# Storing finished tiles from the rows they are added to, and moving a weight tile by 448 bytes, in a four-mixer hybrid layer

## Chip, cores and metric

The kernel runs on one core of one Trainium2 chip. The metric is the device time of one execution in microseconds (us). Three executions of the kernel before took 1055.12 to 1059.49 us, with a median of 1059.02.

## What is computed

One layer over 2,048 tokens of width 1,024, in float32. After an RMS norm a projection gives 13 slices of 256 columns, which four mixers use: dilated attention (A), a gated MLP over chunks (B), pooling (C) and retention (D). Each mixer's output is gated, the four are joined, projected back, normed and added to the input rows:

```python
h = _rms_norm(x, pre_g)
proj = jnp.einsum('bsd,de->bse', h, w_in)
aq, ak, av, ag, bu, bv, bg, cx, cg, dq, dk, dv, dg = jnp.split(proj, N_IN_SLICES, axis=-1)
...
y = jnp.concatenate([ya * jax.nn.silu(ag), yb * jax.nn.silu(bg),
                     yc * jax.nn.silu(cg), yd * jax.nn.silu(dg)], axis=-1)
y = jnp.einsum('bse,ed->bsd', y, w_out)
return x + _rms_norm(y, post_g).astype(x.dtype)
```

## The kernel before

Each float32 product is made of three TensorE matmuls: both operands are split into a high and a low part, and high·high, high·low and low·high are summed in the same accumulator.

**Projections and mixers (0 to 682 us).** The normed rows are transposed into `hh` (high) and `hl` (low), for groups of 512 tokens. `weights()` loads a slice of `w_in` and splits it. Two forms use it. `proj_t` (matmuls into `ps_t`) holds 128 columns of weights in the array and streams 512 tokens of `hh` or `hl`. `proj_m` (into `ps_m`) holds 128 tokens of `hh` or `hl` and streams 256 columns of the weight tile `w256`, in 32 calls of 48 matmuls. `w256` is the first tile of its pool `pa` in the stack of the left side of SBUF; its start there is a multiple of 512 bytes, and the tiles of the pools after it lie behind it.

**Attention (682 to 922 us).** Two pairs of heads. Mixers B, C and D are finished by then, and their outputs lie in DRAM (`yb`). For nine of the 16 tiles of 128 tokens, `partial(t)` already projects these three mixers' six blocks: it loads them as `yraw`, `split_y` makes the stationary tiles `yt` from them, 36 matmuls go into `ps_out`, ScalarE copies the result to `z`, and `z` is stored in DRAM as `partd`. The `issue_after` marks at the end of the program spread the nine calls over the second pair of heads. `yt`, `yraw` and `z` of these calls lie in pool `p3` on the right side of SBUF, which is filled from the top down; there `yt` starts 32 bytes past a multiple of 64, and in `p4` on a multiple of 64.

**Tail (922 us to the end).** `combine` finishes the attention's part (`ya`, and its low and high parts `ysa`). Then `final(t)` runs once for each tile. Tiles 0 to 8 load the stored half sum into `z` (pool `p4`, name `z4`, four buffers), project the remaining two blocks with 12 matmuls, and VectorE adds `z` to the accumulator (L868). Tiles 9 to 15 are projected whole, 48 matmuls. The order is three whole ones, then mixed. For every tile the input rows are loaded into `xr` (three buffers), ScalarE squares and sums (L869), a chain of small VectorE operations gives the reciprocal root, VectorE scales the accumulator into `z` (L875), GpSimd adds the input rows (L877; for the last tile VectorE, in halves), and SyncE stores `z` (L878). The matmuls' stationary blocks `yt` of tile 9 lie in `p3`, those of tiles 10 to 15 in `p4`.

SyncE issues every DMA, in program order: a load that must wait for a buffer holds up all that stand behind it on that queue. The order of each engine's instructions comes from a scheduler that works with estimated durations; pools and their buffer counts set which waits it adds. Where a buffer is written again, the writer waits for the last reader, a store among them.

The two pools' names in the text: `pa` on the left in the projections, `p3` on the right from the attention on. `cp` holds constants, `p2` the attention's small tiles. Two tiles named `align0` and `align1` hold no data and only fill space.

Of the kernel before, what the change touches and what calls it, by code (L numbers as in the profile page):

```python
# [9 lines left out]
F32 = mybir.dt.float32  # L10
# [4 lines left out]
ALU = mybir.AluOpType  # L15
# [3 lines left out]
P = 128  # L19
SEQ = 2048  # L20
DM = 1024
# [67 lines left out]
def hymba(ctx: ExitStack, tc: tile.TileContext, x, pre_g, w_in, sgu_g, sgu_w, sgu_b, pool_w,  # L89
          pool_scale, ret_g, w_out, post_g, cmix, catt, out, dbg=None, npart=9, spread=(0.3, 0.95)):  # L90
    nc = tc.nc
    V, A, G, T, D = nc.vector, nc.scalar, nc.gpsimd, nc.tensor, nc.sync
# [10 lines left out]
    cp = ctx.enter_context(tc.tile_pool(name="const", bufs=1))  # L103
# [15 lines left out]
    ya_d = [scratch(f"ya{g}", [P, 2, GRP]) for g in range(NG)]  # L119

    ident = cp.tile([P, P], F32, name="ident")
    cp.tile([P, 96], F32, name="align0")
    for _ in range(2):
        small.tile([P, 8], F32, tag="align1", name="align1")

# [22 lines left out]
    with ExitStack() as c1:  # L148
# [42 lines left out]
        W2 = 6  # L191
        hT = {}
        first = []

        def prologue(gs, step):

# [43 lines left out]
        def weights(col, n, eng=V, scales=(1.0,)):  # L240

            if n == P:
                w = p1.tile([P, 2, KT, n], F32R, tag="w128", bufs=3, name="w128")
            else:
                w = pa.tile([P, 2, KT, n], F32R, tag="w256", bufs=1, name="w256")
            kc = KT * P // n
            for k in range(0, KT, kc):
                raw = p1.tile([P, kc, n], F32, tag="raw", bufs=2, name="raw")
                D.dma_start(raw, w_src[:, k:k + kc, col:col + n])
                for i, sc in enumerate(scales):  # L250
                    cs = slice(i * n // len(scales), (i + 1) * n // len(scales))
                    hi, lo = w[:, 0, k:k + kc, cs], w[:, 1, k:k + kc, cs]
                    A.activation(hi, raw[:, :, cs], AF.Copy, scale=sc)  # L253
                    if sc == 1.0:
                        eng.tensor_tensor(lo, raw[:, :, cs], r32(hi), ALU.subtract)  # L255
                    else:
                        V.scalar_tensor_tensor(lo, raw[:, :, cs], sc, r32(hi), ALU.mult, ALU.subtract)
            return w
# [301 lines left out]
    def attention(p, tab):  # L560
        o01 = (big if p == 0 else po).tile([P, 2, SEQ], F32, tag="big" if p == 0 else "o01", name="att_o01")
        o2 = po.tile([P, SEQ], F32, tag="o2", name="att_o2")
        o = [o01[:, 0], o01[:, 1], o2]
        wt = pc.tile([P, 3, 2, 2, 2, 8], F32, tag="wt", bufs=1, name="wt")
        for s in range(2):
            h = 2 * p + s
            rows = slice(s * HD, (s + 1) * HD)
            other = slice((1 - s) * HD, (2 - s) * HD)
            q2 = pm.tile([P, SEQ], F32R, tag="m8", bufs=7, name="q2")
            k2a = pm.tile([P, SEQ], F32R, tag="m8", bufs=7, name="k2a")  # L570
            k2b = pm.tile([P, SEQ], F32R, tag="m8", bufs=7, name="k2b")
            D.dma_start(r32(q2[rows]), qk_d[0][p][rows, 0])
            D.dma_start(r32(q2[other]), qk_d[0][p][rows, 1])
            for z in (rows, other):
                D.dma_start(r32(k2a[z]), qk_d[1][p][rows, 0])
                D.dma_start(r32(k2b[z]), qk_d[1][p][rows, 1])
            for b, dil in enumerate(DILS):
                vt = pm.tile([P, 16, 2 * HD], F32R, tag="m8", bufs=7, name="att_v")
                dst = r32(vt)
                if dil == 1:  # L580
                    src = v_d[h].rearrange("(n t c) d -> c t n d", c=4, t=32)
                    for c in range(4):
                        D.dma_start(dst[c * 32:(c + 1) * 32], src[c])
                elif dil == 4:
                    D.dma_start(dst.rearrange("q (j c) d -> q j (c d)", j=4),
                                v_d[h].rearrange("(j q c) d -> q j (c d)", j=4, c=4))
                else:
                    D.dma_start(dst.rearrange("q r d -> q (r d)"), v_d[h].rearrange("(q r) d -> q (r d)", r=16))
                qb = q2
                if dil != 1:  # L590
                    qb = pm.tile([P, SEQ], F32R, tag="m8", bufs=7, name="q2b")
                    if dil == 4:
                        src = r32(q2).rearrange("p (j k c i) -> p c j k i", j=4, c=4, i=8)
                        dst = qb.rearrange("p (j c k i) -> p c j k i", j=4, c=4, i=8)
                        for c in range(4):
                            (V if c < 3 else G).tensor_copy(dst[:, c], src[:, c])
                    else:
                        V.tensor_copy(qb.rearrange("p (r w i) -> p r w i", r=16, i=8),
                                      r32(q2).rearrange("p (w r i) -> p r w i", r=16, i=8))
                if dil == 1:  # L600
                    sv = p2.tile([P, 3, 2, 16], F32, tag="sv", bufs=2, name="sv")
                    raw = p2.tile([64, P], F32, tag="sT", bufs=1, name="sraw")
                    D.dma_start(raw, st_d[h].rearrange("b z (n q) -> (b z n) q", q=P))
                    branch(h, dil, qb, k2a, k2b, vt, tab, o[b], sv[:, b])
                    weigh(sv, raw, wt[:, :, :, s])
                    continue
                st = p2.tile([P, 2, 16], F32, tag="stat", bufs=2, name="att_st")
                branch(h, dil, qb, k2a, k2b, vt, tab, o[b], st)
                keep_stats(h, b, dil, st)
        return o01, o2, wt  # L610
# [203 lines left out]
    def load_y(t, pool):  # L814
        raw = pool.tile([P, 6, P], F32, tag="yraw", bufs=2, name="yraw")
        D.dma_start(raw, yb_d[t // 4][:, t % 4])
        return raw

    def split_y(raw, pool, eng):

        ys = []
        for e in range(0, 6, 3):
            yt = pool.tile([P, 3, 2, P], F32R, tag="yt", bufs=2, name="yt")
            src = raw[:, e:e + 3]
            if eng is A:
                A.activation(yt[:, :, 0], src, AF.Copy)
            else:
                eng.tensor_copy(yt[:, :, 0], src)
            G.tensor_tensor(yt[:, :, 1], src, r32(yt[:, :, 0]), ALU.subtract)
            ys += [yt[:, j] for j in range(3)]  # L830
        return ys
# [12 lines left out]
    def partial(t):  # L844
        z = p3.tile([P, DM], F32, tag="z", bufs=2, name="z")
        ys = split_y(load_y(t, p3), p3, G)
        for n in range(2):
            A.activation(z[:, n * GRP:(n + 1) * GRP], out_proj(ys, range(2, 8), n, ps2, "part"), AF.Copy)
        D.dma_start(part_d[t * P:(t + 1) * P], z)

    def final(t, have, yb, py, p4, ps4, tag, post_b, last):
        tt = slice((t % 4) * P, (t % 4 + 1) * P)
        ys, es = [ya[e][t // 4][:, :, tt] for e in range(2)], (0, 1)
        z = p4.tile([P, DM], F32, tag="z4", bufs=4, name="z4")
        if have:
            D.dma_start(z, part_d[t * P:(t + 1) * P])
        else:
            ys, es = split_y(yb or load_y(t, p4), py, A) + ys, (2, 3, 4, 5, 6, 7, 0, 1)
        xr = p4.tile([P, DM], F32, tag="xr", bufs=3, name="xr")
        D.dma_start(xr, x[0, t * P:(t + 1) * P])  # L860
        ss = small.tile([P, 16], F32, tag="ss", name="ss2")[:, :2]
        sq = p4.tile([P, DM], BF16, tag="sq", bufs=2, name="sq")
        halves = [slice(n * GRP, (n + 1) * GRP) for n in range(2)]
        banks = []
        for n, ns in enumerate(halves):
            ps = out_proj(ys, es, n, ps4, tag)
            if have:
                V.tensor_tensor(ps, ps, z[:, ns], ALU.add)  # L868
            A.activation(sq[:, ns], ps, AF.Square, scale=DM ** -0.5, accum_out=ss[:, n:n + 1])  # L869
            banks.append(ps)  # L870
        V.tensor_scalar(ss[:, :1], ss[:, :1], ss[:, 1:], EPS, ALU.add, ALU.add)
        rstd = small.tile([P, 16], F32, tag="rstd", name="rstd2")[:, :1]
        rsqrt(rstd, ss[:, :1], 1)
        for ps, ns in zip(banks, halves):
            V.scalar_tensor_tensor(z[:, ns], ps, rstd, post_b[:, ns], ALU.mult, ALU.mult)  # L875
        for ns in halves if last else [slice(0, DM)]:
            (V if last else G).tensor_tensor(z[:, ns], z[:, ns], xr[:, ns], ALU.add)  # L877
            D.dma_start(out[0, t * P:(t + 1) * P, ns], z[:, ns])  # L878

    po = ctx.enter_context(tc.tile_pool(name="po", bufs=1, side="right", reuse_waits="tile"))  # L880
    pc = ctx.enter_context(tc.tile_pool(name="pc", bufs=1, side="right", reuse_waits="tile"))
# [64 lines left out]
```

## Time and profile before

| what | value |
| --- | --- |
| time, median of three runs | 1059.02 us (1055.12 to 1059.49) |
| time of the profiled execution | 1055.14 us |
| its span | 1053.4 us |
| its granted TensorE clock, mean | 0.981 of full |
| TensorE busy | 1000.1 us (95%), 5,960 matmuls |
| VectorE busy | 519.1 us (49%) |
| ScalarE busy | 376.4 us (36%) |
| GpSimd busy | 228.0 us (22%) |

All views are of one execution; times in them count from the start of its span. A row of a timeline has its start, its length, the engine, the line of the code, the operation, output and input tiles, the shape and the number of instructions that the row joins; in brackets stands how long the engine was idle before it and what ended the idle time. Matmuls overlap, so the pace of a row of n is its length less that of the last, over n − 1, or the distance of two starts. A row of waits has the total, the number and the longest. SPq is SyncE's queue of DMA issues; a DMA's own row in the chain of work runs from its issue to its landing.

### The profile page before, as it was taken

How to read it: one execution, taken by the hardware profiler on the slowest of the kernel's cores; microseconds unless marked ns; L12 is line 12 of the kernel's file. 1: busy time of each engine (PE TensorE's matmuls, PEld its weight loads, DVE VectorE, ACT ScalarE, POOL GpSimd, SP SyncE). 2: the span in 40 equal slices, each digit the busy share in tenths (PEclk: the TensorE clock that was granted, in tenths of full speed). 3: DMA queues.
4: the chain of work that ended last, by engine and by line, in shares of the span. 5: the costliest groups of instructions: out<-in, count | busy, mean ns of one | idle time of the engine just before them, and what ended most of it. 6: DMA issues, size and time to landing. Idle time of an engine off the chain costs nothing.

```text
span 1053.4 us, 15825 instructions
## 1 busy us (share of the span) xinstructions
PE 1000.1 (95%) x5960; PEld 861.6 (82%) x5960; DVE 519.1 (49%) x1584; ACT 376.4 (36%) x871; POOL 228.0 (22%) x217
## 2 busy tenths in 40 slices
PE   5899999999999999999999999988999989899994
PEld 5889898998888998989898888777896979776773
DVE  7621215687323331031666222176876667727776
ACT  6320313132212431031221111297873878612231
POOL 2310002221133000002120124031116411313444
PEclk9999999999999999999999999996999989989998
DMA  7530222332423232040310661187474663445565
GB/s 284 146 100 21 81 80 81 121 107 72 123 68 103 91 95 65 1 140 34 128 61 21 154 179 41 62 219 203 102 212 141 161 202 77 154 142 181 175 250 220
DMA packets 110988, 128.91 MB, mean 122 GB/s; under 512 B 9888, under 2 KB 88992, under 8 KB 108864
## 3 DMA queue, kind: packets, MB, share of 16 engines
q1 hardware_dynamic: 110912, 127.90, 39.7%
q8 instruction: 47, 0.77, 0.3%
q14 instruction: 29, 0.24, 0.1%
HBM read 91.57 MB, written 36.31 MB: 121 GB/s over the span
## 4 chain that ended last, share of the span: by engine, by line
PE 82%; DMA 7%; DVE 6%; ACT 2%; issue 2%; POOL 1%; SPq 1%; DVEq 0%; POOLq 0%; ACTq 0%
PE ps_t L98 38%; PE ps_m L98 16%; PE ps_out L98 10%; PE ps_s L98 4%; PE ps_o L98 4%; PE ps_pt L101 3%; PE ps_of L98 2%; DMA out_dram<-z 2%; DMA k2b<-qk 2%; DMA cm<-in_cmix_dram 1%; PE ps_in L98 1%; POOL z L877 1%; PE ps_mix L98 1%; DMA raw<-in_w_in_dram 1%; PE ps_x L101 1%
## 5 line engine op out<-in xcount | busy, mean ns | idle before, releaser
L98 PE MATMUL ps_t<-hh,w 128*128 128x512 f32 x1152 | 366.9, 395 | 0.0
L98 PEld LDWEIGHTS ps_t<-hh,w 128*128 128x128 f32 x1152 | 215.9, 188 | 47.8 <-issue 3.4
L98 PE MATMUL ps_t<-hl,w 128*128 128x512 f32 x576 | 226.1, 393 | 0.0
L98 PE MATMUL ps_m<-w,hh 128*128 128x256 f32 x1024 | 190.1, 286 | 1.6 <-ACT hh L235 1.6
L98 PEld LDWEIGHTS ps_m<-w,hh 128*128 128x128 f32 x1024 | 161.3, 193 | 3.3 <-ACT hh L235 2.2
L98 PE MATMUL ps_out<-wo,yt 128*128 128x512 f32 x576 | 153.9, 406 | 0.6 <-DVE z L875 0.6
L98 PE MATMUL ps_m<-w,hl 128*128 128x256 f32 x512 | 147.7, 288 | 0.1
L98 PEld LDWEIGHTS ps_t<-hl,w 128*128 128x128 f32 x576 | 108.3, 188 | 23.2 <-issue 1.4
L98 PEld LDWEIGHTS ps_out<-wo,yt 128*128 128x128 f32 x576 | 105.6, 192 | 23.1 <-issue 2.8
L255 DVE TENSOR_TENSOR w<-raw,w 128x1024 fp32r<-128x1024 f32 x42 | 58.5, 1402 | 109.5 <-ACT w L253 109.5
L98 PEld LDWEIGHTS ps_m<-w,hl 128*128 128x128 f32 x512 | 98.8, 193 | 0.8 <-DVE hl L236 0.3
L253 ACT ACTIVATE w<-raw 128x1024 fp32r<-128x1024 f32 (+1 forms) x56 | 55.0, 997 | 67.7 <-PE ps_t L98 37.3
L652 DVE CUSTOM_DVE_ANT_0 att_p<-ps_s,tab 128x128 f32<-128x128 f32 (+1 forms) x192 | 60.6, 360 | 36.3 <-PE ps_s L98 29.6
L662 DVE TENSOR_TENSOR pt_lo<-ps_pt,pt_hi 128x512 fp32r<-128x512 f32 x80 | 51.5, 652 | 18.6 <-ACT pt_hi L661 18.2
L654 ACT ACTIVATE att_p<-att_p,att_st 128x128 f32<-128x128 f32 (+1 forms) x128 | 55.0, 433 | 6.9 <-DVE att_st L652 6.4
L98 PE MATMUL ps_o<-pt_hi,att_v 128*128 128x128 f32 (+1 forms) x204 | 53.9, 284 | 1.7 <-DVE att_o L677 1.7
L98 PE MATMUL ps_o<-pt_lo,att_v 128*128 128x128 f32 (+1 forms) x204 | 52.9, 294 | 0.4 <-DVE pt_lo L662 0.4
L101 PE MATMUL ps_pt<-ident,att_p 128*128 128x128 f32 x300 | 50.6, 285 | 2.7 <-ACT att_p L654 2.5
L449 POOL TENSOR_TENSOR d_g<-d_g,ret_b 128x512 f32<-128x512 f32 x8 | 10.4, 1296 | 184.6 <-ACT d_g L447 184.6
L661 ACT ACTIVATE pt_hi<-ps_pt 128x512 fp32r<-128x512 f32 x80 | 44.1, 565 | 12.0 <-PE ps_pt L101 6.4
L98 PEld LDWEIGHTS ps_o<-pt_hi,att_v 128*128 128x128 f32 x204 | 41.0, 201 | 4.3 <-DVE att_o L677 1.9
L877 POOL TENSOR_TENSOR z<-z,xr 128x1024 f32<-128x1024 f32 x15 | 35.8, 2390 | 32.4 <-DVE z L875 27.7
(174 smaller groups left out, 1409.9 us busy)
## 6 DMA issues: line engine op xcount, KB each, us to landing
raw<-in_w_in_dram SPq DMA_DIRECT2D x52, 512.0 KB
qk<-qk_s SPq DMA_DIRECT2D x16, 512.0 KB
att_v<-vd SPq DMA_DIRECT2D x8, 1024.0 KB
xr<-in_x_dram SPq DMA_DIRECT2D x16, 512.0 KB
out_dram<-z SPq DMA_DIRECT2D x15, 512.0 KB
xt<-in_x_dram SPq DMA_DIRECT2D x7, 1024.0 KB
yraw<-yb SPq DMA_DIRECT2D x16, 384.0 KB
partd<-z SPq DMA_DIRECT2D x9, 512.0 KB
```

What stands on the lines that cost most here:

```text
L98: return T.matmul(o, lhsT, rhs, start=start, stop=stop, skip_group_check=True)
L101: T.transpose(o, i, ident[:n, :n])
L253: A.activation(hi, raw[:, :, cs], AF.Copy, scale=sc)
L255: eng.tensor_tensor(lo, raw[:, :, cs], r32(hi), ALU.subtract)
L449: G.tensor_tensor(o, o, ret_b.unsqueeze(1).broadcast_to([P, 2, 256]), ALU.mult)
L652: V.tensor_tensor_reduce(out=pr[:, u, :w], in0=ps[:, u, :w], in1=bb, scale=-SLOPES[h] * HD ** -0.5, scalar=3e38, op0=ALU.add, op1=ALU.min, ...
L654: A.activation(pr[:, u, :w], pr[:, u, :w], AF.Exp, bias=neg, scale=-1.0, accum_out=st[:, 1, n:n + 1])
L661: A.activation(hi, pt[:, :w], AF.Copy)
L662: V.tensor_tensor(lo, pt[:, :w], r32(hi), ALU.subtract)
L877: (V if last else G).tensor_tensor(z[:, ns], z[:, ns], xr[:, ns], ALU.add)
```

## The change

Five things are edited. In `final`, the last add writes its result over `xr`, and the store reads `xr`; `xr` gets a fourth buffer. So a `z` buffer is free after the add, and an `xr` buffer only after the store. In `weights`, 448 bytes are reserved ahead of `w256` and 64 behind it: `w256` now starts 448 bytes past a multiple of 512, and what follows it moves by a whole 512. In `partial`, 480 bytes are reserved in `p3` in its first call, by which tiles of `p3` and of the pools behind it on the right side move down; `yt` there now starts on a multiple of 512. The attention's `sv` takes the place of the pad `align0`, of the same size, with one buffer instead of two.

```diff
     ident = cp.tile([P, P], F32, name="ident")
-    cp.tile([P, 96], F32, name="align0")
+    svs = cp.tile([P, 3, 2, 16], F32, name="sv")
...
             else:
+                if not align:
+                    align.append(pa.tile([P, 112], F32, name="align2"))
                 w = pa.tile([P, 2, KT, n], F32R, tag="w256", bufs=1, name="w256")
+                if len(align) == 1:
+                    align.append(pa.tile([P, 16], F32, name="align3"))
...
-                    sv = p2.tile([P, 3, 2, 16], F32, tag="sv", bufs=2, name="sv")
+                    sv = svs
...
         ys = split_y(load_y(t, p3), p3, G)
+        if t == 0:
+            p3.tile([P, 120], F32, name="align4")
...
-        xr = p4.tile([P, DM], F32, tag="xr", bufs=3, name="xr")
+        xr = p4.tile([P, DM], F32, tag="xr", bufs=4, name="xr")
...
-            (V if last else G).tensor_tensor(z[:, ns], z[:, ns], xr[:, ns], ALU.add)
-            D.dma_start(out[0, t * P:(t + 1) * P, ns], z[:, ns])
+            (V if last else G).tensor_tensor(xr[:, ns], z[:, ns], xr[:, ns], ALU.add)
+            D.dma_start(out[0, t * P:(t + 1) * P, ns], xr[:, ns])
```

Up to the last microseconds of the attention every engine keeps its order of instructions. From there on, SyncE's queue has another. This is SyncE early in the tail, before; the number in a name tells the tiles of one name apart, in the order in which they are made, `z4` is `z` of `final`, and the tiles stored are those of the first finals:

```order
L878 DMA out_0_dram<-z4_9119 128x1024
L860 DMA xr_9379<-in_x_dram 128x1024
L878 DMA out_0_dram<-z4_9205 128x1024
L860 DMA xr_9426<-in_x_dram 128x1024
L816 DMA yraw_9883<-yb3_76 128x768
L856 DMA z4_9377<-partd_77 128x1024
L856 DMA z4_9424<-partd_77 128x1024
L856 DMA z4_9471<-partd_77 128x1024
```

And the same place now (the `xr` load of the fourth tile, `xr_9378`, stands 9 rows ahead of the first row shown):

```order
L885 DMA out_0_dram<-xr_9125 128x1024
L821 DMA yraw_9882<-yb3_76 128x768
L867 DMA xr_9425<-in_x_dram 128x1024
L885 DMA out_0_dram<-xr_9211 128x1024
L867 DMA xr_9472<-in_x_dram 128x1024
L863 DMA z4_9376<-partd_77 128x1024
L863 DMA z4_9423<-partd_77 128x1024
L863 DMA z4_9470<-partd_77 128x1024
```

Before, the three `z` loads need the stores of `z4_9119`, `z4_9205` and a later one; now they need adds only, but `xr_9425` ahead of them is loaded into the buffer of `xr_9125`, and `xr_9472` into that of `xr_9211`, both of which are stored just before.

This is SyncE's queue shortly before its end, before the change; only the last stores follow:

```order
L860 DMA xr_9891<-in_x_dram 128x1024
L878 DMA out_0_dram<-z4_9788 128x1024
L860 DMA xr_9972<-in_x_dram 128x1024
L856 DMA z4_9970<-partd_77 128x1024
L856 DMA z4_10017<-partd_77 128x1024
L878 DMA out_0_dram<-z4_9835 128x1024
L860 DMA xr_10019<-in_x_dram 128x1024
L878 DMA out_0_dram<-z4_9882 128x1024
L860 DMA xr_10073<-in_x_dram 128x1024
```

And now:

```order
L867 DMA xr_9890<-in_x_dram 128x1024
L867 DMA xr_9971<-in_x_dram 128x1024
L885 DMA out_0_dram<-xr_9789 128x1024
L867 DMA xr_10018<-in_x_dram 128x1024
L863 DMA z4_9969<-partd_77 128x1024
L885 DMA out_0_dram<-xr_9836 128x1024
L863 DMA z4_10016<-partd_77 128x1024
L885 DMA out_0_dram<-xr_9890 128x1024
L867 DMA xr_10072<-in_x_dram 128x1024
```

The names shift by one (`z4_9970` is now `z4_9969`). Before, the two last `z` loads follow one another, behind one `xr` load, and `z4_10017` takes the buffer of `z4_9788`. Now `xr_10018` takes the buffer of `xr_9789`, whose store stands right ahead of it, and a store lies between the two `z` loads.

More of the change, by code (lines that the diff above doesn't have):

```diff
@@ L193, in hymba @@
         first = []
+        align = []
         def prologue(gs, step):
```

## The prediction

> **What bounds the kernel now.** I read the head of the page first, then the chain of work that ended last, then a table of busy time by stage, and only then single waits.
>
> ```profile
> span 1053.4 us, 15825 instructions
> PE 82%; DMA 7%; DVE 6%; ACT 2%; issue 2%; POOL 1%; SPq 1%; DVEq 0%; POOLq 0%; ACTq 0%
> core 0: us, PE busy (x) PEld busy (x) DVE busy (x) ACT busy (x) POOL busy (x), PEclk, DMA share, GB/s
> 265.00:450.00 185.00, 184.82 (x1024) 160.19 (x1025) 49.77 (x68) 44.96 (x65) 23.64 (x31) 1.00 0.26 76
> 724.00:922.00 198.00, 187.66 (x1227) 166.02 (x1226) 146.07 (x498) 144.64 (x434) 57.93 (x65) 0.97 0.53 151
> 955.00:1054.00 99.00, 79.97 (x344) 63.09 (x342) 70.92 (x229) 23.16 (x68) 43.78 (x23) 0.95 0.60 215
> ```
>
> Three stages with three limits. In the projections (265 to 450 as a sample) TensorE is busy 184.82 of 185 us: whatever one matmul gains or loses there is gained or lost by the kernel. In the attention (724 to 922) it is busy 187.66 of 198. In the tail of output projections (955 to 1054) it is busy 80 of 99 and no engine is full, so there the waits decide. The waits of that stretch, and its end:
>
> ```profile
> DVE ps_out L868 <- DMA z<-partd: 15.7, 5, 5.8
> PE ps_out L98 <- DVE z L875: 3.4, 4, 2.0
> 1039.63 0.39 PE L98 MATMUL ps_out<-wo,ysa 128*128 128x512 f32 x1
> 1036.66 1.30 DVE L868 TENSOR_TENSOR ps_out<-ps_out,z 128x512 f32<-128x512 f32 x2 [5.07 <-DMA z<-partd]
> 1038.47 1.30 DVE L868 TENSOR_TENSOR ps_out<-ps_out,z 128x512 f32<-128x512 f32 x2 [0.52 <-DMA z<-partd]
> 1042.16 1.41 DVE L875 SCALAR_TENSOR_TENSOR z<-ps_out,rstd,post_b 128x512 f32<-128x512 f32 x2
> 1047.39 1.41 DVE L875 SCALAR_TENSOR_TENSOR z<-ps_out,rstd,post_b 128x512 f32<-128x512 f32 x2
> 1048.71 1.28 DVE L877 TENSOR_TENSOR z<-z,xr 128x512 f32<-128x512 f32 x2
> ```
>
> The last matmul is done at 1040.0, yet the span ends 13.4 us later. VectorE sat 5.07 us until the stored half sum of a tile (`z<-partd`) was back at 1036.66; from there it works nearly without a gap (adds, reciprocal roots, scalings, last adds) until 1050, and the last store ends the span. So the end hangs on when that load of `z` lands. Why it landed so late stands on the queue:
>
> ```profile
> 1028.87 0.34 SPq L878 DMA_DIRECT2D out_dram<-z  x1
> 1029.25 2.14 SPq L860 DMA_DIRECT2D xr<-in_x_dram  x1
> 1031.48 2.00 SPq L856 DMA_DIRECT2D z<-partd  x2
> 1033.58 0.38 SPq L878 DMA_DIRECT2D out_dram<-z  x1
> 1028.87 4.24 DMA out_dram<-z
> ```
>
> SyncE issues all transfers in program order. The two `z` loads begin at 1031.48, and the second can only follow when the store issued at 1028.87 has landed (28.87 + 4.24 = 1033.11), as its buffer is that store's source. The first took 1036.66 − 1031.48 = 5.2 us to land, the second 1038.47 − 1033.1 = 5.4.
>
> **The change part by part.**
>
> *Stores from `xr`.* Now the add frees `z`, and only the store's landing frees `xr`. The `z` load itself therefore no longer waits for a store, but the `xr` load does, and in the new program each pair of `z` loads is queued behind an `xr` load that needs the latest store landed. At the end the order becomes: store of tile A (the one issued at 1028.87), `xr` load into A's own buffer, first `z` load, store of the next tile, second `z` load. The `xr` load cannot go before 1033.11. Its own issue takes what such a row takes when nothing holds it:
>
> ```profile
> 1034.01 0.42 SPq L860 DMA_DIRECT2D xr<-in_x_dram  x1
> 1043.70 4.83 POOL L877 TENSOR_TENSOR z<-z,xr 128x1024 f32<-128x1024 f32 x2 [9.59 <-DVE z L875]
> 1031.72 2.39 POOL L877 TENSOR_TENSOR z<-z,xr 128x1024 f32<-128x1024 f32 x1 [0.34 <-DVE z L875]
> ```
>
> So the first `z` load goes at 1033.5 instead of 1031.48, and by 5.2 us lands at 1038.7 instead of 1036.66: +2.0. The second stands behind the store of the tile whose add GpSimd ends at 1031.72 + 2.39 = 1034.1, goes at 1034.5 and by 5.4 lands at 1039.9 instead of 1038.47: +1.4. VectorE needs both in turn, hence between +1.4 and +2.0 at the end. Against that, what comes before may be early: the loads of the first four `xr` rows are issued before the tail begins, and the first three `z` loads are then free of stores of their own. Of VectorE's 15.7 us of waiting for `z` some would go, and only as far as TensorE, 80 of 99 us busy, is not at once in the way again. A gain there is bounded by the wait that an early `z` hands on to TensorE, the 3.4 us row, of which I give half to the four loads that are ahead: −1.7. I take **+1.5**, with −1.7 to +3.4 (a second round of +1.4 on top of +2.0) as bounds. Same work, same instruction shapes: the add writes another buffer, at GpSimd's 2.4 us as before.
>
> *Start of the weight tile in `pa`.* `w256` is the moving operand of `ps_m`. Its start goes from a multiple of 512 bytes to 448 past one; the tiles behind it all move by a whole 512. Count and pace:
>
> ```profile
> L98 PE MATMUL ps_m<-w,hh 128*128 128x256 f32 x1024 | 190.1, 286 | 1.6 <-ACT hh L235 1.6
> L98 PE MATMUL ps_m<-w,hl 128*128 128x256 f32 x512 | 147.7, 288 | 0.1
> 383.29 41.73 PE ps_t L98 x184
> 425.02 23.03 PE ps_m L98 x192
> ```
>
> 1,536 such matmuls at 23.03 / 192 = 120 ns each, in a stage that TensorE fills. The neighbour `ps_t`, twice as wide, takes 41.73 / 184 = 226.8. The difference of the two is 106.8 ns for 256 columns; what is left, 13.2 ns, is the same in both, although `ps_t` streams a tile at another place. So the row shows a fixed cost and none of the start: **0**. Bounds: if the new start brought it to half of a `ps_t`, 113.4 ns, −6.6 × 1,536 = −10.1 us; if it cost what a start off the grid costs in the next item, 8 ns, +12.3 us.
>
> A rule that bears on the size of that gain is in the Trainium skill, "TensorE: Matmul & The Clock Gate", section Back-to-back issue gap: columns over 2.4 GHz and about 2.5 ns, so some 109 ns for 256 columns. The 120 ns here do not agree; by the page the gain could be an estimated 11 ns × 1,536 = 17 us, if the start were what keeps `ps_m` from it.
>
> *480 bytes in `p3`.* All tiles of the right side but the first few move down by 480 bytes; `yt`, the stationary operand of the half sums, from 32 past a multiple of 64 to a multiple of 512.
>
> ```profile
> 913.92 4.42 PE L98 MATMUL ps_out<-wo,yt 128*128 128x512 f32 x18
> 957.04 4.28 PE L98 MATMUL ps_out<-wo,yt 128*128 128x512 f32 x18
> 993.43 4.24 PE L98 MATMUL ps_out<-wo,yt 128*128 128x512 f32 x18
> L98 PE MATMUL ps_out<-wo,yt 128*128 128x512 f32 x576 | 153.9, 406 | 0.6 <-DVE z L875 0.6
> ```
>
> Taking 0.39 us for the last of each run, as the row at 1039.63 has it, the first (a half sum, `yt` in `p3`) goes at (4.42 − 0.39) / 17 = 237 ns, the other two (`yt` in `p4`, on the grid already) at 229 and 226.5. The middle one, like the first, starts behind narrow matmuls, so 8 to 10 ns are the start's. Of the 576, six tiles of 36 lie in `p4`; 360 are in `p3`: 360 × 8 = −2.9 us if all of it lies on the path. 198 − 187.66 = 10.3 us of idle in that stage says that not all does. I take **−2.0**, bounds 0 and −3.8.
>
> The same skill, "SBUF — State Buffer", section Who interferes with whom, gives TensorE two independent read ports, one for the moving operand and one for weight loads, and says that it never waits on anyone. By that the place of `yt` would cost nothing and this term would be 0; 237 against 229 ns speaks for the term.
>
> *Small ones, 0.*
>
> ```profile
> 687.19 1.03 POOL L891 CAST sel<-sel_raw 32x1024 fp32r<-32x1024 f32 x1 [27.38 <-ACT att_p L654]
> 692.15 0.95 POOL L828 CAST yt<-yraw 128x384 fp32r<-128x384 f32 x2 [3.93 <-DMA yraw<-yb]
> ```
>
> `sv` in one buffer: a head fills it only when the head before it has long been weighed, on VectorE in order; without that cover it would be one wait per head. GpSimd's copy of `sel` gets two more waits, on transfers; it ends at 688.2 and GpSimd then idles 3.93 us for a load, which hides them. The fourth `xr` buffer adds no instruction.
>
> **The sum.** 1055.14 us, the time of the profiled execution (its span 1053.4 and 1.7 around it), + 1.5 − 2.0 + 0 = 1054.6. That execution was the fast end of the three shown; the median lies 3.9 higher, at 1059.02. The same step from there is **1058.5 us**. About 0.5%, 5.3 us, is what a measurement of this kernel can tell from no change, so this is no change. Adding the bounds without the weight tile's gives −5.5 to +3.4, 1053.5 to 1062.4.
>
> **The rivals.**
>
> *A, the tail gets shorter.* Two rows for its price, a scaling and the last square:
>
> ```profile
> 1044.65 1.40 DVE L875 SCALAR_TENSOR_TENSOR z<-ps_out,rstd,post_b 128x512 f32<-128x512 f32 x2
> 1040.99 0.60 ACT L869 ACTIVATE sq<-ps_out 128x512 bf16<-128x512 f32 x1
> ```
>
> If the freed `z` buffers let the last two loads land before TensorE ends, VectorE's chain starts not at 1036.66 but with the last matmul: from the end of the last tile's matmuls at 1040.0, one square (0.6), the root and the scaling, which from one tile's scaling to the next's are 1047.39 − 1044.65 = 2.74, then scaling, adds and store as now (1053.4 − 1047.39 = 6.0): 1049.3, −4.1, and up to 3.4 more when TensorE's waits go as well: −4 to −7.5, with the `yt` term −6 to −9.5: about 1051. For it: the 15.7 us of waits. Against: the queue is in order, and an `xr` load that needs a store still stands ahead of them. 25%.
>
> *B, the weight tile's old start is what holds `ps_m`.* −10.1, with the other terms −10.6: 1048. For it: the 13 ns that no column explains, and that `yt` shows a start to matter at all. Against: `ps_t` has the same 13 ns. 10%.
>
> *C, the new wait of the `xr` loads decides (slower).* VectorE waits for `z` in five stretches; if in each the `z` loads go 2.0 us later, as worked out for the last, and TensorE's eight accumulators are full by then so that nothing is caught up, that is 5 × 2.0 = +10.0, with the `yt` term +8.0: 1067. It decides from the point at which TensorE's 3.4 us of waits for the scaling grow with every round. For it: the order of the queue. Against: TensorE has 19 us of slack in that stretch. 12%.
>
> *D, the new start of the weight tile costs (slower).* +12.3 − 0.5: 1071. For it: `yt`'s 8 ns. Against: 448 is a multiple of 64, which `yt`'s old place was not. 8%.
>
> **How the numbers follow.** Forecast 45%, A 25%, B 10%, C 12%, D 8%. Faster by over 0.5% is A and B, 35%; within 0.5% the forecast, 45%; slower C and D, 20%. The range leaves out less than two in ten: at 1046 it cuts off the better half of B, 5%; at 1066 D and half of C, 14%. The forecast's own range is 1053.5 to 1062.4.
>
> **What would show it.** `ps_m` in the chain at 23.0 us for 192 (21.8 would be B, 24.6 D). Half sums' runs of 18 at 4.28 instead of 4.42. In the tail, each `z` load's issue right behind an `xr` load that stood until a store landed, VectorE's last wait for `z` ending about 2 us later against the last matmul, and its total near 15.7 us: under 8 would be A, over 22 C. The forecast is wrong if `ps_m`'s pace moves by over 2 ns, or if TensorE's end and the span's end come closer than 9 us.

## The result, and the profile after

The changed kernel takes 1050.76 us, the median of five runs (1048.79 to 1052.46), against 1059.02 for the kernel before; the ratio is 0.9928, with a 95% interval of 0.9905 to 0.9951. So it is faster by 8 us, 0.7%. The forecast was no change, 1058.5 us, in a range of 1046 to 1066. The time lies in that range, but below the 1053.5 to 1062.4 that the forecast's own terms span.

The profiled execution took 1048.79 us, its span 1047.1, 6.3 us shorter than that of before. Where these 6.3 us lie is read from the first and last start of three groups of matmuls. First the kernel before (duration least, median and most in ns, then first and last start in us):

```profile
L98 PE MATMUL ps_t<-hh,w x1152: 386/390/792, 47.2 to 681.4; 128*128 128x512 f32 x192
L98 PE MATMUL ps_o<-pt_lo,att_v x204: 222/280/416, 689.0 to 913.8; 128*128 128x128 f32 x54, 128*128 128x256 f32 x48
```

The same groups of the changed kernel, and its span:

```profile
span 1047.1 us, 15841 instructions
L98 PE MATMUL ps_t<-hh,w x1152: 387/389/791, 46.8 to 675.9; 128*128 128x512 f32 x192
L98 PE MATMUL ps_o<-pt_lo,att_v x204: 220/279/415, 683.5 to 906.7; 128*128 128x128 f32 x54, 128*128 128x256 f32 x48
```

The projections run from 46.8 to 675.9 instead of 47.2 to 681.4: 5.1 us less. The attention takes 906.7 − 683.5 = 223.2 instead of 224.8: 1.6 less. The tail, from there to the end, takes 1047.1 − 906.7 = 140.4 instead of 139.6: 0.8 more. Attention and tail are near the forecast's −2.0 and +1.5, but differences of this size say little: in the kernel with only the weight tile moved (below) the same two stretches take 223.0 and 141.8 us, though nothing in them was edited. The projections were forecast at 0.

What moved in the projections stands in the chain of work. The prediction shows one run of 192 of the kernel before, 23.03 us; the next one there is this:

```profile
471.54 23.23 PE ps_m L98 x192
```

The changed kernel, same places:

```profile
93.64 22.61 PE ps_m L98 x192
139.71 21.97 PE ps_m L98 x192
379.92 41.73 PE ps_t L98 x184
421.65 22.61 PE ps_m L98 x192
467.72 21.97 PE ps_m L98 x192
```

`ps_t` has kept its 226.8 ns. `ps_m` went from 23.03 to 22.61 us in one run of 192, 2.2 ns a matmul, and from 23.23 to 21.97 in the next, 6.6 ns. From start to start, all runs that long have 120.0 ns before; now some have 117.8 and some 113.4. The mean over all `ps_m` matmuls that follow one another falls from 119.8 to 115.8, which is 6 us in 1,536; 5.1 of them show in the stage.

The end of the tail, by queue, VectorE and TensorE, and the wait that the prediction named:

```profile
1019.40 0.34 SPq L885 DMA_DIRECT2D out_dram<-xr  x1
1023.22 0.33 SPq L867 DMA_DIRECT2D xr<-in_x_dram  x1
1023.64 0.38 SPq L863 DMA_DIRECT2D z<-partd  x1
1024.11 0.38 SPq L885 DMA_DIRECT2D out_dram<-xr  x1
1024.55 0.42 SPq L863 DMA_DIRECT2D z<-partd  x1
...
1029.17 1.30 DVE L875 TENSOR_TENSOR ps_out<-ps_out,z 128x512 f32<-128x512 f32 x2 [6.08 <-DMA z<-partd]
1031.27 0.21 DVE L878 TENSOR_SCALAR ss<-ss 128x1 f32<-128x1 f32 x1 [0.80 <-ACT sq L876]
1032.08 1.29 DVE L875 TENSOR_TENSOR ps_out<-ps_out,z 128x512 f32<-128x512 f32 x2
1041.05 1.41 DVE L882 SCALAR_TENSOR_TENSOR z<-ps_out,rstd,post_b 128x512 f32<-128x512 f32 x2
1042.37 1.28 DVE L884 TENSOR_TENSOR xr<-z,xr 128x512 f32<-128x512 f32 x2
...
1031.22 0.84 PE L98 MATMUL ps_out<-wo,ysa 128*128 128x512 f32 x3
...
DVE ps_out L875 <- DMA z<-partd: 15.9, 3, 7.1
```

This is the mechanism of the first term, row by row. A store is issued at 1019.40; SyncE then stands until 1023.22, for the `xr` load behind it wants that store's buffer and waits for its landing; only then do the two `z` loads go, with a store between them. VectorE waits 6.08 us for the first. SyncE's waits for stores from 955 us to the end, first before and then now (total, number, longest), say the same:

```profile
SPq L856 <- DMA out_dram<-z: 5.3, 4, 1.7
SPq L867 <- DMA out_dram<-xr: 32.3, 12, 4.7
```

Before, four loads of `z` waited for stores, 5.3 us in all; now twelve loads of `xr` do, 32.3 us in all.

The last matmul ends at 1032.1 and the span 15.0 us later, where it was 13.4: 1.6 us more. From the second of the two last adds to the end of the span it is 15.0 us in the changed kernel (1032.08 to 1047.1) and 14.9 before (1038.47 to 1053.4). So the 1.6 us are that add: it starts with the end of the last matmul, where it started 1.5 us ahead of it before. Its load is not the whole reason. By the completion marks of the trace, the second `z` load landed at 1031.5, 0.5 us ahead of the last matmul's end, against 1.6 us before (1038.4): 1.1 us of the 1.6. The rest is VectorE's own order, which has changed here too: the first tile's root steps, which waited 0.80 us for ScalarE's square, now stand between the two adds.

### The profile page after: what moved, and what is told of

The parts are those of the page before. It is cut to its first block, busy times and chain, and to the rows that moved or that the text cites. A ratio compares the mean times of both kernels' runs of the same rounds, so it can differ in the third digit from the quotient of the medians.

```text
span 1047.1 us, 15841 instructions
## 1 busy us (share of the span) xinstructions
PE 991.7 (95%) x5960; PEld 855.2 (82%) x5960; DVE 516.9 (49%) x1584; ACT 376.0 (36%) x871; POOL 229.9 (22%) x217
## 4 chain that ended last, share of the span: by engine, by line
PE 81%; DMA 9%; DVE 5%; POOL 2%; issue 1%; ACT 1%; SPq 1%; DVEq 0%; ACTq 0%; POOLq 0%
PE ps_t L98 38%; PE ps_m L98 15%; PE ps_out L98 13%; PE ps_s L98 3%; PE ps_o L98 3%; PE ps_of L98 2%; PE ps_pt L101 2%; DMA k2b<-qk 2%; DMA ret_b<-in_ret_g_dram 1%; PE ps_in L98 1%; DMA ya<-ysa 1%; DMA wo_raw<-in_w_out_dram 1%; DVE z L882 1%; DMA z<-partd 1%; PE ps_mix L98 1%
## 5 line engine op out<-in xcount | busy, mean ns | idle before, releaser
L98 PE MATMUL ps_m<-w,hh 128*128 128x256 f32 x1024 | 184.3, 282 | 1.8 <-ACT hh L236 1.8
L98 PEld LDWEIGHTS ps_m<-w,hh 128*128 128x128 f32 x1024 | 157.5, 189 | 3.6 <-ACT hh L236 2.4
L98 PE MATMUL ps_m<-w,hl 128*128 128x256 f32 x512 | 145.5, 284 | 0.2 <-DVE hl L237 0.2
L884 POOL TENSOR_TENSOR xr<-z,xr 128x1024 f32<-128x1024 f32 x15 | 37.9, 2533 | 34.2 <-DVE z L882 21.6
```

What stands on the lines that cost most here:

```text
L98: return T.matmul(o, lhsT, rhs, start=start, stop=stop, skip_group_check=True)
L884: (V if last else G).tensor_tensor(xr[:, ns], z[:, ns], xr[:, ns], ALU.add)
```

## Experiments

Every ratio is against the kernel before, executed in the same session on the same chip. It is an estimate over all executions, 4 to 12 of each edited kernel and 12 to 23 of the kernel before, and differs a little from the quotient of the two medians.

| run | median us | before | ratio, 95% interval |
| --- | --- | --- | --- |
| weight tile's start alone | 1050.97 | 1057.62 | 0.9941, 0.9918 to 0.9965 |
| right side and sv | 1051.83 | 1057.62 | 0.9955, 0.9935 to 0.9974 |
| stores from xr alone | 1055.00 | 1057.62 | 0.9981, 0.9960 to 1.0002 |
| weight tile and right side, no stores from xr | 1047.34 | 1058.47 | 0.9901, 0.9873 to 0.9929 |
| weight tile by 256 bytes | 1059.67 | 1058.47 | 1.0008, 0.9988 to 1.0028 |
| hh, hl and wo by 64 bytes | 1050.12 | 1058.47 | 0.9926, 0.9902 to 0.9951 |
| the changed kernel again | 1050.71 | 1058.47 | 0.9939, 0.9911 to 0.9967 |
| sv alone | 1053.92 | 1059.42 | 0.9951, 0.9934 to 0.9968 |
| changed, z loads on ScalarE | 1044.18 | 1059.42 | 0.9855, 0.9828 to 0.9881 |
| weight tile by 192 and right side | 1047.17 | 1059.42 | 0.9886, 0.9862 to 0.9911 |
| weight tile and sv | 1049.44 | 1056.13 | 0.9928, 0.9899 to 0.9956 |

Wherever the right side or `hh` and `hl` move, `sv` is in the constants as well. The groups that are compared differ in their granted clock as well. Among the executions of the kernel before, 0.001 more of it goes with about 0.7 us less (0.71 and 0.73 us in the two groups of 23). The nine executions with `sv` alone have a mean of 0.9796 and those of before beside them 0.9769; the four with the `z` loads on ScalarE have 0.9828. Whether the edits raise the clock or the executions had it by chance is not shown. If it was chance, an estimated 2 us of the gain of `sv` and 4 us of that of the `z` loads go with it.

The theory at the start was that the weight tile's new place brought the gain, with the tail as forecast; the rival, that the freed `z` buffers in the tail brought it.

**The weight tile alone.**

```diff
+                if not align:
+                    align.append(pa.tile([P, 112], F32, name="align2"))
                 w = pa.tile([P, 2, KT, n], F32R, tag="w256", bufs=1, name="w256")
+                if len(align) == 1:
+                    align.append(pa.tile([P, 16], F32, name="align3"))
```

> Only the weight tile's start moves, by 448 bytes. Theory (the start sets the pace of the 1,536 ps_m matmuls): the two runs of 192 in the chain at 22.6 and 22.0 us as in the changed kernel instead of 23.0 and 23.2, the attention begins 5.5 us earlier, the time falls by 5 to 6 us (ratio 0.9945). Rival (the stores from xr brought the gain): ps_m at 120 ns, time within 1 us of before.

It has the changed kernel's pace, 22.61 and 21.97 us, and 0.9941, 6.2 us less; the attention begins 4.5 us earlier, where 5.5 was expected. The theory stands: this one edit is most of the gain.

**The right side, with sv.**

```diff
-    cp.tile([P, 96], F32, name="align0")
+    svs = cp.tile([P, 3, 2, 16], F32, name="sv")
...
+        if t == 0:
+            p3.tile([P, 120], F32, name="align4")
```

> Only the 480 bytes on the right side, with sv in the pad's place, without which they do not fit. Theory: nothing moves up to 682 us, half sums' matmuls at 227 to 229 ns instead of 234 to 237, the attention stage 1 to 2 us shorter, the time 1 to 2.5 us less (ratio 0.998 to 0.999). Rival (the place of yt costs nothing): no difference in the attention stage beyond 0.5 us.

0.9955, 4.8 us less, more than either theory had. The half sums became faster, here a run of 18 in the kernel with the right side moved:

```profile
910.19 4.32 PE L98 MATMUL ps_out<-wo,yt 128*128 128x512 f32 x18
```

(4.32 − 0.39) / 17 = 231 ns instead of 237, some 2 us in 360. These quotients hold the longer first step of a run. From start to start, all half-sum matmuls of the stage that follow one another go from 232.8 to 230.0 ns, which is 1.0 us in 360; 227 to 229 was expected. The rest was put down to `sv`, which the prediction had at nothing; see below.

**The stores from xr alone.**

```diff
-        xr = p4.tile([P, DM], F32, tag="xr", bufs=3, name="xr")
+        xr = p4.tile([P, DM], F32, tag="xr", bufs=4, name="xr")
...
-            (V if last else G).tensor_tensor(z[:, ns], z[:, ns], xr[:, ns], ALU.add)
-            D.dma_start(out[0, t * P:(t + 1) * P, ns], z[:, ns])
+            (V if last else G).tensor_tensor(xr[:, ns], z[:, ns], xr[:, ns], ALU.add)
+            D.dma_start(out[0, t * P:(t + 1) * P, ns], xr[:, ns])
```

> Only the stores from xr and its fourth buffer. Theory: nothing changes up to 914 us; in the tail the loads of xr wait for stores instead of the loads of z, and the end comes 0 to 1.5 us later against the last matmul of the attention (ratio 1.000 to 1.0015). Rival (the freed z buffers brought the gain): time 4 to 7 us less (ratio 0.994 to 0.996).

0.9981, with an interval that just holds 1: 2 us less, if anything, so neither the theory's cost nor the rival's gain is shown. The order of SyncE's queue is not that of the changed kernel: the last `z` loads stand ahead of the last `xr` loads here. That the same edit makes another order when `sv` is moved as well is what the later runs turn on.

**Starts alone.** A stream of matmuls in the kernel's pattern, one moving and one stationary start after another.

```python
for t2 in range(2):
    for j in range(2):
        tt = slice((t2 * 2 + j) * P, (t2 * 2 + j + 1) * P)
        o = acc[:, j * 256:(j + 1) * 256]
        for k in range(8):
            mm(o, hv[0][:, k, tt], wv[:, 0, k], k == 0, False)
            mm(o, hv[0][:, k, tt], wv[:, 1, k], False, False)
            mm(o, hv[1][:, k, tt], wv[:, 0, k], False, k == 7)
```

> A stream of matmuls alone: it leaves out the whole layer and stores zeros and one accumulator. Groups of 96 with 256 moving columns and of 72 with 512, in the kernel's pattern of three, at one moving and one stationary start after another, and all once more in reverse order. Theory A (the start of the moving rows alone): 256 columns at 120 ns with starts that are multiples of 512, 113 to 118 ns at 448, whatever the stationary start; theory B (the distance of the two reads): 448 with 448 as slow as 0 with 0, and stationary starts move the pace as moving ones do; theory C (what ran before sets a phase): the two passes over the same start differ as much as the starts do.

The table of busy time for ten stretches of 10 us shows how many matmuls touch each. In order, as moving start and stationary start in bytes: with 256 columns 192 and 0, 256 and 0, 448 and 0, 512 and 0, 0 and 64, 448 and 448; with 512 columns 0 and 0, 448 and 0, 0 and 32, 448 and 448:

```profile
114.55:124.55 10.00, 10.00 (x90) 1.00 0.00 0
125.79:135.79 10.00, 10.00 (x85) 1.00 0.01 2
161.01:171.01 10.00, 10.00 (x86) 1.00 0.00 0
184.35:194.35 10.00, 10.00 (x85) 1.00 0.01 2
219.12:229.12 10.00, 10.00 (x90) 1.00 0.00 0
265.04:275.04 10.00, 10.00 (x85) 1.00 0.00 0
276.88:286.88 10.00, 10.00 (x45) 1.00 0.01 2
395.34:405.34 10.00, 10.00 (x44) 1.00 0.00 0
446.74:456.74 10.00, 10.00 (x44) 1.00 0.01 2
531.60:541.60 10.00, 10.00 (x45) 1.00 0.01 2
```

The starts of single matmuls give the pace more finely (ns from start to start, past the first 24 of a group, the two passes together; the very first group of the run, 143.9 ns, is left out):

| moving, stationary start | 256 columns | 512 columns |
| --- | --- | --- |
| 0, 0 | 120.0 | 226.7 |
| 256, 0 and 0, 256 | 120.0 (first alone) | 226.7 |
| 448, 448 | 120.0 | 226.7 |
| 64, 0 | 117.8 | 228.9 |
| 128, 0 | 120.0, then 118.6 | 232.4 |
| 0, 64 | 113.3 | 233.3 |
| 192, 0 | 113.3 | not run |
| 448, 0 | 117.8 | 233.3 |
| 0, 448 | 113.3 | 229 |
| 0, 32 | 118.4 | 233.3 |

Theory B: the start of neither operand counts by itself, but the distance of the two, modulo 256 bytes. At distance 0, the narrow matmuls have their worst pace and the wide ones their best: 448 with 448 is as 0 with 0. At other distances the stream shows that the distance alone does not settle the narrow pace: 192 with 0 and 960 with 0 gave 113.3 and 448 with 0 gave 117.8, each in both passes, though all three are 192 modulo 256. Most starts gave the same in both passes; 16 with 0 gave 113.3 and 118.7, as theory C would have it. What settles the rest is not shown.

**Two tests of that in the kernel.** The weight tile by 256 bytes, still at distance 0:

```diff
+                    align.append(pa.tile([P, 64], F32, name="align2"))
                 w = pa.tile([P, 2, KT, n], F32R, tag="w256", bufs=1, name="w256")
+                    align.append(pa.tile([P, 64], F32, name="align3"))
```

> Only the weight tile moves, by 256 bytes instead of 448. Theory B (the distance of the moving and the stationary start, counted modulo 256): ps_m stays at 120 ns, 23.0 and 23.2 us for 192, time within 1 us of before (ratio 0.999 to 1.001). Theory A (any start off a multiple of 512 helps): 22.0 to 22.6 us for 192 and 5 us less.

It changed nothing, 1.0008, and the chain has the old pace to the last digit:

```profile
426.21 23.03 PE ps_m L98 x192
472.72 23.23 PE ps_m L98 x192
```

And the weight tile where it was, but `hh` and `hl` by 64 bytes:

```diff
-    cp.tile([P, 96], F32, name="align0")
+    cp.tile([P, 16], F32, name="align5")
+    svs = cp.tile([P, 3, 2, 16], F32, name="sv")
...
+    small.tile([P, 56], F32, tag="align6", name="align6")
```

> The weight tile's start stays where it was, modulo 512; instead hh and hl, and with them the output weights that follow in the same buffers, move by 64 bytes (sv in the constants, to make room). They are the stationary side of ps_m and the moving side of ps_t. Theory B (the distance decides): ps_m at 113 to 118 ns although its moving start is unchanged (21.8 to 22.6 us for 192), and ps_t, whose distance was 0, slower, 228.9 instead of 226.7 (184 in 42.1 us instead of 41.7), so -3.4 to -10.2 on ps_m, +3.9 on ps_t and +0.9 on the output projections: -5 to +1.5 us. Theory A (the moving start alone): ps_m at 120 ns, and ps_t slower all the same: +5 us.

```profile
94.67 21.78 PE ps_m L98 x192
380.82 42.11 PE ps_t L98 x184
422.93 22.61 PE ps_m L98 x192
```

The narrow matmuls became faster though their moving start is the old one, and the wide ones slower, 42.11 / 184 = 228.9 ns, the stream's number. Theory A falls. The time, 0.9926, is 8 us less, beyond the expected −5 to +1.5; this kernel has `sv` in the constants too.

**Adding up, and the tail.** Both moves without the stores from `xr` (the changed kernel with the lines below as they were before), and the changed kernel on the same chip:

```diff
-        xr = p4.tile([P, DM], F32, tag="xr", bufs=4, name="xr")
+        xr = p4.tile([P, DM], F32, tag="xr", bufs=3, name="xr")
...
-            (V if last else G).tensor_tensor(xr[:, ns], z[:, ns], xr[:, ns], ALU.add)
-            D.dma_start(out[0, t * P:(t + 1) * P, ns], xr[:, ns])
+            (V if last else G).tensor_tensor(z[:, ns], z[:, ns], xr[:, ns], ALU.add)
+            D.dma_start(out[0, t * P:(t + 1) * P, ns], z[:, ns])
```

> Both moves, of the weight tile and of the right side, without the stores from xr. Theory (the two starts add up and the stores from xr cost something beside them): ps_m's runs of 192 at 22.6 and 22.0 us, half sums at 227, time 8 to 9 us under before (ratio 0.9915 to 0.9925), 1 to 2 us under the changed kernel in the same call. Rival (the stores from xr bring 1.5 to 2 us here as well): 1.5 to 2 us over the changed kernel.

> The changed kernel once more, on the same chip and in the same rounds as the kernel with both moves but without the stores from xr. Its ratio to before should come out near 0.993 again. If the stores from xr cost time once the rest is faster, this kernel is 1 to 2 us slower than the one without them; if they save time, as their single run hints (ratio 0.9981, 0.9960 to 1.0002), it is 2 us faster.

Without the stores from `xr` the kernel takes 1047.34 us, with them 1050.71: 3.4 us more by the medians. The two intervals overlap, but the ends of the profiled executions do not. This is the span without the stores from `xr`, and its last matmuls:

```profile
span 1044.9 us, 15824 instructions
1033.62 0.84 PE L98 MATMUL ps_out<-wo,ysa 128*128 128x512 f32 x3
```

The end comes 10.5 us after the last matmul, against 15.0 and 15.3 in the two profiled executions of the changed kernel. The next run takes the supposed cause away: the changed kernel with the `z` loads on ScalarE's queue.

```diff
-            D.dma_start(z, part_d[t * P:(t + 1) * P])
+            A.dma_start(z, part_d[t * P:(t + 1) * P])
```

> The changed kernel, with the nine loads of the half sums into z issued by ScalarE instead of SyncE, so that they no longer stand behind the loads of xr that wait for stores; all else on SyncE keeps its order. Theory (the z loads behind the waiting xr loads are what the stores from xr cost): VectorE's wait for z falls from 15.9 us to under 8, the end comes 11 to 13 us after the last matmul instead of 15.4 to 15.7, time 2 to 4 us under the changed kernel (ratio to before 0.990 to 0.992). Rival (the transfers themselves are late, whoever issues them): ratio 0.993 to 0.995 as before, and the wait stays over 12 us.

```profile
1016.36 0.35 ACTq L863 DMA_DIRECT2D z<-partd  x1
1017.84 0.33 ACTq L863 DMA_DIRECT2D z<-partd  x1
1026.59 1.29 DVE L875 TENSOR_TENSOR ps_out<-ps_out,z 128x512 f32<-128x512 f32 x2 [2.17 <-DMA z<-partd]
1038.33 1.28 DVE L884 TENSOR_TENSOR xr<-z,xr 128x512 f32<-128x512 f32 x2
1031.66 0.84 PE L98 MATMUL ps_out<-wo,ysa 128*128 128x512 f32 x3
DVE ps_out L875 <- DMA z<-partd: 7.5, 3, 3.2
```

The last two `z` loads go at 1016.36 and 1017.84 instead of 1023.64 and 1024.55, VectorE's wait for `z` is 7.5 us (15.9 in the one profile of the changed kernel, 9.2 in the other), and the span, 1043.0, ends 10.5 us after the last matmul (1032.5) instead of 15.0. The ratio is 0.9855, against 0.9928 and 0.9939 for the changed kernel, measured apart from it: some 8 us less, more than the 2 to 4 expected, of which the granted clock may hold a part. So it is the place of the `z` loads in the queue that costs the changed kernel its longer end. This version beats the kernel before and the changed one. That the early `z` buffers are worth anything beyond that is not shown: the end, 10.5 us, is that of the kernel without the stores from `xr`, the two intervals overlap, and `z` loads on ScalarE with the old stores were not run.

**sv.** Its edit alone, and beside the weight tile's:

```diff
-    cp.tile([P, 96], F32, name="align0")
+    svs = cp.tile([P, 3, 2, 16], F32, name="sv")
...
-                    sv = p2.tile([P, 3, 2, 16], F32, tag="sv", bufs=2, name="sv")
+                    sv = svs
```

> Only sv in the pad's place with one buffer, which the prediction priced at nothing. No start of a matmul operand moves, but the queue of SyncE in the tail gets another order by it: the last half sum's store and an output weight's load go behind three loads of xr, and ya0 ahead of them. Theory (the order brought what the two moves do not explain): the end comes 11 to 12 us after the last matmul instead of 13.3, time 1.5 to 2.5 us under before (ratio 0.9975 to 0.9985), with the half sums still at 234 to 237 ns. Rival (it is nothing, and the right side's move alone made 4 us): within 0.5 us of before.

> The weight tile's move and sv in the pad's place; the right side stays and the stores stay with z. Between the weight tile's move alone (0.9941 of before) and both moves with sv (0.9901). If sv's order is worth the 3 to 5 us that its own run hints, and the right side 0 to 1 us: ratio 0.990 to 0.991. If sv is worth 1 to 2 us and the right side 2 to 3: 0.992 to 0.993. The half sums at 234 to 237 ns and the end 11 to 12 us after the last matmul in either case.

Alone it gives 0.9951, 5.2 us less, over twice what was expected. Beside the weight tile it gives 0.9928 against 0.9941 without, 1.4 us less; with the clock's share taken off, as above, the two would be an estimated 3.3 and 2.6. From the other side, the right side's move is worth 0.9955 against 0.9951 beside `sv` alone, nothing, and 0.9901 against 0.9928, 2.9 us, where the weight tile has moved as well. The intervals are 0.2 to 0.3% each way: what is shown is that `sv`'s edit is not free of effect, between 1 and 5 us, and that with the right side it brings 4 to 5. What the two share is an order: with `sv` in the constants the last half sum's store and a load of output weights stand behind three `xr` loads in SyncE's queue, and no start of an operand has moved. Before, and with `sv` alone:

```profile
919.00 0.32 SPq L849 DMA_DIRECT2D partd<-z  x1
919.42 0.38 SPq L553 DMA_DIRECT2D wo_raw<-in_w_out_dram  x1
921.19 1.81 SPq L860 DMA_DIRECT2D xr<-in_x_dram  x3
...
917.76 1.58 SPq L860 DMA_DIRECT2D xr<-in_x_dram  x3
920.85 0.33 SPq L849 DMA_DIRECT2D partd<-z  x1
921.53 0.33 SPq L553 DMA_DIRECT2D wo_raw<-in_w_out_dram  x1
```

The profiled execution with `sv` alone shows little of a gain: the end came 12.5 us after the last matmul instead of 13.4, where 11 to 12 was expected, and that execution, at 1056.5 us, was the slowest of its nine. The other profiled executions bear out a shorter end: 10.5 to 11.6 us in the five further kernels with `sv` in the constants and stores from `z`, 12.8 to 13.4 in the three without (the kernel before, the weight tile alone, the weight tile by 256). In the two pairs of kernels that differ by `sv` alone it is 0.9 and 1.3 us; where the rest of what the medians say comes from stays open.

**The weight tile by 192.**

```diff
-                    align.append(pa.tile([P, 112], F32, name="align2"))
+                    align.append(pa.tile([P, 48], F32, name="align2"))
```

> Both moves without the stores from xr, the weight tile 192 bytes past a multiple of 512 instead of 448. The same distance modulo 256, so by theory B the same choice of two paces, 113.3 or 117.8 ns: 21.8 to 22.7 us for 192, time within 2 us of the kernel with 448 (ratio to before 0.988 to 0.992). If 192 is the better start, as the stream alone had it (113.3 against 117.8), 21.8 us in all four runs of 192 and 3 us less.

0.9886, with the same 22.61 and 21.97 us for 192 as at 448. The same distance modulo 256, the same two paces; the stream's 113.3 at 192 is had in some runs of the kernel only, as at 448. What chooses between 113.3 and 117.8 was not found.

## Why the prediction failed where it did

**The whole.** The range held, the reason did not. The forecast was no change, within 0.5%; the time fell by 0.7%, and `ps_m`'s pace moved by 2.2 and 6.6 ns, over the 2 ns at which the prediction called itself wrong. The time came within 1 us of rival A's "about 1051", but not by its mechanism: A's shorter tail did not come, and half of rival B's gain did. That the sum of the other terms came out near is luck in part, as said below.

**The weight tile: 0 forecast, −5.1 measured.** The step that failed is "what is left, 13.2 ns, is the same in both […]. So the row shows a fixed cost and none of the start". That the remainder is the same in both is no finding: the 106.8 ns for 256 columns was itself taken as the difference of the two paces, and so 120.0 − 106.8 and 226.8 − 2 × 106.8 must be equal, whatever the paces are. Nothing in the rows could tell a fixed cost from one of the start. What the runs showed in its place: both forms ran at the pace of distance 0 from their stationary operand, `ps_m` with its worst, 120.0, and `ps_t` with its best, 226.7; at the new start `ps_m` has 113.4 and 117.8. The range's lower bound for it, −10.1, held: that was 113.4 ns throughout, and the kernel has it about half the time. Rival B, with a chance of 10%, was so nearest to the mechanism, at half its size; what holds `ps_m` is the distance from the stationary start, not the weight tile's start alone.

The argument against rival D, that 448 is a multiple of 64 and `yt`'s place was not, was the wrong ground for the right side: a distance of 64 bytes, or of 448, costs the wide matmuls 2.2 to 6.6 ns in the stream.

**The skill's rule.** The Trainium skill, "TensorE: Matmul & The Clock Gate", section Back-to-back issue gap, gives some 109 ns for 256 columns, by a formula that it calls that of an isolated matmul; of a stream of weight loads and matmuls, which `ps_m` is, it says that both set the spacing, and so the estimate of 17 us took the formula further than the Trainium skill does. The best that any start gave here was 113.3 ns. The Trainium skill, "SBUF — State Buffer", section Who interferes with whom, has two independent read ports for TensorE and says that it never waits on anyone. Here the pace of one stream depends on the distance of its two reads, 113.3 against 120.0 ns with all else equal. By that one would expect no such thing; the measurement decides, and it does not show whether a port is the cause.

**The right side: −2.0 forecast, about −1 by the pace of its matmuls.** The direction held: 231 ns instead of 237 in the run of 18 (4.28 us forecast, 4.32 measured), and 2.8 ns from start to start over the stage. The 8 ns a matmul were too many. The −1.6 us of the attention's stage cannot be put down to it, as the kernel with the weight tile alone has −1.8 there. By whole runs it lies between 0 and −2.9 us.

**The tail: +1.5 forecast, +0.8 from the last `ps_o` on and +1.6 from the last matmul to the end.** The mechanism, an `xr` load that stands for the latest store with the `z` loads behind it, is shown by the rows, by SyncE's 32.3 us of waits and by the run that takes the `z` loads out of its way. Its size is less sure: the two `z` loads landed some 0.5 and 1.1 us later against the last matmul, where 2.0 and 1.4 were forecast, and VectorE's changed order, which the forecast did not have, makes up the rest of the 1.6. VectorE's total wait for `z`, 15.9 us as forecast, was 9.2 in the second profile of the same kernel, so that this sign says nothing. What the forecast had wrong as well is its assignment: it took the whole new order to come from the stores from `xr`. Alone they gave another order and at most a gain, 0.9981; the changed kernel's order needs `sv`'s edit as well, and beside it the stores from `xr` cost 3.4 us. The +1.5 thus stands for a gain by `sv` and a cost of the stores, neither of which was in the sum by itself.

**`sv`: forecast at 0.** The step asked whether a head would wait for the buffer, and did not ask what the allocation does to the scheduler's order in the tail. Measured: a gain of 1 to 5 us.

**Rivals.** A, a tail shorter by 4 to 7.5 us through the freed buffers, did not come in the changed kernel. With the `z` loads out from behind the `xr` loads the end is 4.5 us shorter than in the changed kernel, but no shorter than without the stores from `xr`. C and D did not come.

## What to carry to other kernels

A buffer that is freed early is of no use while the transfer that wants it is queued behind one that waits for something else: look at what stands ahead of the load in its queue before pricing the buffer. Where TensorE is full, the distance of the moving and the stationary start, modulo 256 bytes, is worth trying for each form of matmul by itself; 0 was best for 512 columns and worst for 256. An edit that only moves memory can change a scheduler's order far away, so edits of one change are to be measured alone and together. And a remainder that was computed from two rows cannot confirm itself on the same two rows.

## What was not expected of the hardware

The best and the worst pace of both forms lie 6.7 ns apart, 113.3 and 120.0 for 256 columns, 226.7 and 233.3 for 512. That is what 16 columns cost at the 106.8 ns for 256. What lies between is no mixture of the two: at 117.8 the single distances are 117 to 119 ns, at 228.9 they are 225 to 232. At one and the same start the kernel has long runs at 113.4 and others at 117.8.
